# Ordering a two-layer encoder kernel at build time with operation times from a timeline simulator

## The chip, the cores and the metric

The kernel runs on one core of one Trainium2 chip. The metric is the time of one execution on the device, in microseconds (us), given as the median of several runs. Smaller is better.

## What is computed

Two layers of a hybrid bidirectional encoder for one sequence of 512 tokens (S) of width 1024 (DM), and a final RMSNorm. One layer, cut from the reference to what matters:

```
xn = rmsnorm(x, g1)
h  = xn @ W_in                       # one projection, split among four mixers
A  = gated DeltaNet, both directions: short conv + silu, l2norm(q), l2norm(k);
     chunks of 64 tokens: t_mat = I + strict_lower(k_beta k^T * decay)
     u, w = triangular_solve(t_mat, v_beta), triangular_solve(t_mat, k_beta*exp(gc))
     scan over the chunks:  v_new = u - w S
                            o = (q*exp(g)) S + a v_new
                            S = S*exp(g_last) + k_dec^T v_new
     o = rmsnorm(o) * silu(z)
B  = differential attention, two softmax maps per head
C  = windowed grouped-query attention with sinks
D  = bidirectional mLSTM, chunked
y  = sum_b sigmoid(xn @ W_gate_b) * (mixer_b @ W_branch_b)
x  = x + y @ W_out
x  = x + relu(rmsnorm(x) @ W1)^2 @ W2
```

## The kernel before

**Dense products.** Every large product is made of three passes on TensorE (PE): high part by high part, low by high, high by low. A weight block arrives by DMA on SyncE's queue in `wr`; `emit_split` (L288) has ScalarE (ACT) cast its high part into `wh` (L298) and VectorE (DVE) subtract to get the low part `wl` (L299). The activations are split in the same way (`split`, L228 on ACT and L229 on DVE). The passes stand at L398 to L400 (weights stationary, 128x256), L412 to L414 and L441 to L443 (activations stationary) and, for the MLP, L727 to L729 and L790 to L843. Their results lie in `pd`, four banks of PSUM; those of the mixers lie in `pm`, four others.

**Mixers.** A mixer is a Python generator that emits small steps. Mixer A (L1157) inverts the triangular matrices by doubling, in four pairs of groups for each layer, and scans the chunks beside it. The work of one pair, in order of dependence:

- the head: row masks `rm` on GpSimd (POOL, L1257), outer products on PE (L1261, L1263), 16 exponentials on ACT (L1267), DVE (L1272, L1274), POOL (L1273), a cast on ACT (L1276), POOL (L1277), the first block products (L1283, L1285 on DVE, L1286 on POOL), and a copy of the identity into `Q` on POOL (L1293);
- six levels: PE L1296, DVE `Q` (L1297), PE L1302 and L1304, ACT `DY` (L1306, L1307), and so to the next level;
- the tail: PE L1311, L1312, DVE `R` (L1314), ACT `q` (L1316), POOL (L1317), PE L1321, L1323, ACT `dXY` (L1325, L1326), POOL `Y` (L1328), PE L1333, DVE (L1335), PE L1339, DVE (L1340).

The scan's steps are: POOL `vb`, `kd` (L1356, L1358) and `S` (L1373), PE L1363 and L1366 (state times keys and queries), DVE L1368 to L1370, PE L1378, ACT `vn` (L1380), PE L1386 and L1396, DVE `S` (L1391) and `oc` (L1403, L1405), POOL `oc` (L1406). After the scan `head_norm` (L1134) normalizes each block of 128 tokens (POOL L1138, DVE L1140, POOL L234, DVE L1142, L1143), and `y_T` (L1146) turns it by PE (L1149).

**What sets the order.** Three things. First the order in which the program is written: `fill` (L332) takes steps from the list of dense products for as long as a table of estimated costs says, each time a mixer has emitted a step (`drive`, L347); `lockstep` (L360) takes turns among the parts of mixer A.

```
    def fill(ns):
        debt[0] += ns
        while debt[0] > 0:
            r = step()
```

Second the pools: a buffer that is still read holds up what would write it. Third the framework's scheduler, inside `tile.TileContext`. It plays the whole program at build time with an assumed duration for every operation, and puts on each engine's queue what is ready first; of what is ready, what was written earlier goes first. The result is a fixed queue for each engine, with semaphore waits. On the chip an engine takes its queue strictly in order.

**The start.** `Norm.stats` (L472 to L478) and the transposes L493 prepare the first activations. `pre` (L1094) loads small constants of a layer: `dl` (L1103), the sinks, and `cw`, the weights of the short conv, by five transfers on SyncE's queue (L1117), which DVE halves at L1119.

The change touches only the line that opens the context:

## Time and profile before

| what | before |
|---|---|
| time, median of 3 runs | 2335.07 us (2334.0 to 2337.8) |
| time of the profiled execution | 2333.33 us |
| its span, first to last instruction | 2331.6 us |
| mean granted clock of TensorE | 0.997 |
| busy: PE | 2255.5 us, 97% of the span |
| busy: DVE | 1605.4 us, 69% |
| busy: ACT | 1237.9 us, 53% |
| busy: POOL | 773.6 us, 33% |

The profile shows one execution. For each instruction, or run of like instructions, it gives the start and the duration in us, the engine, the line of the kernel, what is written and read, and in brackets how long the engine was idle before it and which engine or transfer ended that. Matmuls are pipelined: the duration of one is longer than the distance from its start to the next start, and only that distance is what the engine needs for one. A granted clock of 1.00 is 2.4 GHz, 0.50 is 1.2 GHz.

### The profile page before, as it was taken

The numbers are of one execution on the slowest core, as the hardware profiler recorded it, in microseconds if no ns is written. First come the engines' busy times: TensorE is split into PE (matmuls) and PEld (weight loads), VectorE is DVE, ScalarE is ACT, GpSimd is POOL, SyncE is SP. The second block draws the span as 40 slices with busy tenths as digits, with TensorE's granted clock in tenths as the row PEclk, the third lists the DMA queues.
The fourth block names the chain that finished last, engine by engine and source line by source line (L and its number), as shares of the span: only waits on it lengthen the run. The fifth ranks groups of instructions, "written<-read, shape, count | busy, mean of one in ns | idle before, by whom it ended". The sixth has DMA issues, their size and how long they took to land. (4 is left out here: it accounts for less than half of the span.)

```text
span 2331.6 us, 41278 instructions
## 1 busy us (share of the span) xinstructions
PE 2255.5 (97%) x15944; PEld 2014.0 (86%) x15944; DVE 1605.4 (69%) x2944; ACT 1237.9 (53%) x2827; POOL 773.6 (33%) x819
## 2 busy tenths in 40 slices
PE   7999999989999999999999999999999999999998
PEld 6879977878788989999987799878777889899998
DVE  5775547697885477677767745487877854877775
ACT  4565444766765264444445654367576633534443
POOL 1046552032332034443201655412313310444341
PEclk9999999999999999999999999999999999999999
DMA  6322131122122523233323112211322234233322
GB/s 154 94 53 64 56 95 60 55 92 81 56 66 83 162 73 120 90 104 115 107 80 91 55 56 64 91 55 55 100 73 64 64 113 136 88 99 109 100 83 91
DMA packets 234772, 200.81 MB, mean 86 GB/s; under 512 B 31824, under 2 KB 223696, under 8 KB 234576
## 3 DMA queue, kind: packets, MB, share of 16 engines
q1 hardware_dynamic: 231552, 193.09, 27.6%
q10 hardware_dynamic: 2304, 4.20, 0.5%
q8 instruction: 125, 2.05, 0.4%
q0 software_dynamic: 720, 0.89, 0.2%
q14 instruction: 71, 0.58, 0.1%
HBM read 190.25 MB, written 8.39 MB: 85 GB/s over the span
## 5 line engine op out<-in xcount | busy, mean ns | idle before, releaser
L299 DVE TENSOR_TENSOR wl<-wr,wh 128x512 fp32r<-128x512 f32 x540 | 412.1, 783 | 170.4 <-ACT wh L298 162.6
L298 ACT CAST wh<-wr 128x512 fp32r<-128x512 f32 x540 | 316.7, 620 | 222.9 <-PE pd L442 78.0
L441 PE MATMUL pd<-xh,wh 128*128 128x512 f32 (+1 forms) x768 | 307.9, 402 | 0.5 <-ACT xh L228 0.5
L442 PE MATMUL pd<-xl,wh 128*128 128x512 f32 (+1 forms) x768 | 297.3, 387 | 1.8 <-DVE xl L229 1.8
L443 PE MATMUL pd<-xh,wl 128*128 128x512 f32 (+1 forms) x768 | 298.6, 389 | 0.0
L399 PE MATMUL pd<-wl,hh 128*128 128x256 f32 x896 | 248.9, 278 | 0.0
L400 PE MATMUL pd<-wh,hl 128*128 128x256 f32 x896 | 248.8, 278 | 0.0
L398 PE MATMUL pd<-wh,hh 128*128 128x256 f32 x896 | 248.8, 278 | 0.0
L298 ACT CAST wh<-wq 128x512 fp32r<-128x512 f32 x196 | 115.2, 619 | 221.9 <-PE pd L400 95.4
L299 DVE TENSOR_TENSOR wl<-wq,wh 128x512 fp32r<-128x512 f32 x196 | 181.3, 959 | 13.6 <-ACT wh L298 13.5
L818 POOL TENSOR_TENSOR wq<-wq,wq 128x512 f32<-128x512 f32 x84 | 124.8, 1494 | 163.4 <-DVE wl L299 153.2
L443 PEld LDWEIGHTS pd<-xh,wl 128*128 128x128 f32 x768 | 145.6, 190 | 29.8
L442 PEld LDWEIGHTS pd<-xl,wh 128*128 128x128 f32 x768 | 146.2, 190 | 26.3 <-DVE xl L229 2.8
L399 PEld LDWEIGHTS pd<-wl,hh 128*128 128x128 f32 x896 | 168.7, 188 | 0.0
L400 PEld LDWEIGHTS pd<-wh,hl 128*128 128x128 f32 x896 | 168.7, 188 | 0.0
L398 PEld LDWEIGHTS pd<-wh,hh 128*128 128x128 f32 x896 | 168.2, 188 | 0.0
L441 PEld LDWEIGHTS pd<-xh,wh 128*128 128x128 f32 x768 | 145.8, 190 | 23.4 <-ACT xh L228 0.9
L686 DVE TENSOR_TENSOR x<-pd,x 128x512 f32<-128x512 f32 x124 | 85.1, 689 | 100.6 <-PE pd L400 100.5
L398 PE MATMUL pd<-wh,xh 128*128 128x256 f32 x512 | 149.6, 292 | 0.0
L399 PE MATMUL pd<-wl,xh 128*128 128x256 f32 x512 | 145.0, 283 | 0.0
L400 PE MATMUL pd<-wh,xl 128*128 128x256 f32 x512 | 143.5, 280 | 0.0
L1016 POOL TENSOR_TENSOR r<-r,r 128x512 f32<-128x512 f32 x26 | 36.1, 1390 | 301.3 <-PE pd L443 123.9
(394 smaller groups left out, 6632.6 us busy)
## 6 DMA issues: line engine op xcount, KB each, us to landing
wr<-in_w_in SPq DMA_DIRECT2D x92, 512.0 KB
wr<-in_w_mlp SPq DMA_DIRECT2D x72, 512.0 KB
wr<-in_w_gate SPq DMA_DIRECT2D x64, 512.0 KB
wq<-in_w_mlp SPq DMA_DIRECT2D x56, 512.0 KB
wr<-in_w_branch SPq DMA_DIRECT2D x32, 512.0 KB
wr<-in_w_out SPq DMA_DIRECT2D x16, 512.0 KB
x<-in_x SPq DMA_DIRECT2D x16, 256.0 KB
gsd<-gs ACTq DMA_DIRECT2D x16, 256.0 KB
```

The source lines that it names most:

```text
L298: act.copy(wh[:, k:k + n], raw[:, k:k + n])
L299: dve.tensor_tensor(wl[:, k:k + n], raw[:, k:k + n], f(wh[:, k:k + n]), op=ALU.subtract)
L398: mm(o, th, wh[:, k4, :], start=(kt == 0 and tt % 2 == 0), stop=False)
L399: mm(o, th, wl[:, k4, :], start=False, stop=False)
L400: mm(o, tl, wh[:, k4, :], start=False, stop=(kt == kts - 1 and tt % 2 == 1))
L441: mm(o, w1_, xh[kt][:, sl], start=(kt == 0 and hi_ == 0), stop=False)
L442: mm(o, w1_, xl[kt][:, sl], start=False, stop=False)
L443: mm(o, w2_, xh[kt][:, sl], start=False, stop=last)
L686: dve.tensor_tensor(d, bank.rearrange("p (t c) -> p t c", t=2), d, op=ALU.add)
L818: pool.tensor_tensor(d[:, k:k + 2], x[:, k:k + 2], y[:, k:k + 2], op=op)
L1016: pool.tensor_tensor(t, t, sh, op=ALU.add)
```

## The change

The context is opened with one more argument. It makes the scheduler take the durations that it assumes from the framework's timeline simulator, in place of its default ones.

```diff
--- before.py
+++ after.py
@@ -1738,7 +1738,7 @@
         arrays["in_" + n] = v
         args[n] = nc.dram_tensor("in_" + n, v.shape, mybir.dt.from_np(v.dtype), kind="ExternalInput").ap()
     o = nc.dram_tensor("out_0", (1, S, DM), F32, kind="ExternalOutput").ap()
-    with tile.TileContext(nc) as tc:
+    with tile.TileContext(nc, schedule_with_timeline_sim=True) as tc:
         encoder(tc, args, o)
     r = run_bass_kernel_spmd(nc, [arrays], core_ids=[0])
     return r.results[0]["out_0"]
```

No operation is added or taken away on any engine; what changes is where each stands in the queue of its engine, with the buffers and semaphores that follow from it. Three places show it.

**The start, on DVE.** `nj_32` and `nj_33` are the normalized activations of the fourth block of 128 tokens; `pm_37` holds the turned ones of the second block, `xl_21` gets their low parts, `cw_44` is the conv weights. Before:

```order
L233 TENSOR_SCALAR nv_35_179<-ntot_34_177 128x1
L478 SCALAR_TENSOR_TENSOR nj_32_173<-x_2_96,nr_36_180,g_3_99 128x512
L478 SCALAR_TENSOR_TENSOR nj_33_175<-x_2_96,nr_36_180,g_4_100 128x512
L229 TENSOR_TENSOR xl_21_143<-pm_37_185,xh_19_141 128x4x128
L229 TENSOR_TENSOR xl_22_144<-pm_38_192,xh_20_142 128x4x128
L1099 TENSOR_SCALAR gn_39_209<-gn_39_209 128x128
L1100 TENSOR_SCALAR gn_39_209<-gn_39_209 128x128
L1101 TENSOR_SCALAR gn_39_209<-gn_39_209 128x128
L229 TENSOR_TENSOR xl_21_143<-pm_59_330,xh_19_141 128x4x128
```

With the change:

```order
L1100 TENSOR_SCALAR gn_39_209<-gn_39_209 128x128
L1101 TENSOR_SCALAR gn_39_209<-gn_39_209 128x128
L1114 TENSOR_SCALAR nsink_43_227<-sink_42_225 128x8
L1106 TENSOR_TENSOR dl_40_216<-dl_40_216 128x64 x2
L1119 TENSOR_SCALAR cw_44_229<-cw_44_229 128x60
L233 TENSOR_SCALAR nv_35_179<-ntot_34_177 128x1
L1107 TENSOR_REDUCE nlam_41_218<-dl_40_216 128x1 x2
L229 TENSOR_TENSOR xl_21_143<-pm_59_330,xh_19_141 128x4x128
L1109 TENSOR_SCALAR nlam_41_218<-nlam_41_218 128x1
L478 SCALAR_TENSOR_TENSOR nj_32_173<-x_2_96,nr_36_180,g_3_99 128x512
L478 SCALAR_TENSOR_TENSOR nj_33_175<-x_2_96,nr_36_180,g_4_100 128x512
L229 TENSOR_TENSOR xl_21_143<-pm_37_185,xh_19_141 128x4x128
```

L1119, which reads what the five transfers of L1117 bring, stood eleven rows behind the low part `xl_21<-pm_37` (L229); now it stands ahead of it, and of the norm's L233 and L478. The first L442 on PE reads that low part. On PE the transposes `pm_61` (L493, four matmuls, from `nj_32`) now stand ahead of the first L442; they stood 46 dense matmuls behind it. SyncE now issues the sinks, three transfers of `cw`, `dl`, then the last two of `cw`; it was `dl`, the sinks, five of `cw`.

**The third pair of mixer A, on ACT**, from the exponentials of its head on (layer 0; layer 1 alike). Before:

```order
L1267 ACTIVATE e_423_2702<-pm_422_2699,gcol_159_1009 128x128 x4
L1267 ACTIVATE e_426_2712<-pm_425_2709,gcol_159_1009 128x128 x4
L1267 ACTIVATE e_435_2755<-pm_434_2752,gcol_159_1009 128x128 x4
L1267 ACTIVATE e_437_2763<-pm_436_2760,gcol_159_1009 128x128 x4
L1380 COPY vn_439_2773<-pm_438_2768 128x512
L1276 CAST th_440_2792<-e_423_2702 128x512
L997 COPY vx_356_2174<-pd_392_2504 128x2x128 x2
L1276 CAST th_441_2798<-e_426_2712 128x512
L298 CAST wh_470_2971<-wr_382_2385 128x512 x2
L1380 COPY vn_465_2920<-pm_464_2915 128x512
L298 CAST wh_494_3124<-wr_395_2511 128x512
L1306 CAST DY_450_2841<-pm_466_2934 128x2x64x2
```

With the change:

```order
L1267 ACTIVATE e_423_2702<-pm_422_2699,gcol_159_1009 128x128 x4
L1267 ACTIVATE e_426_2712<-pm_425_2709,gcol_159_1009 128x128 x4
L1267 ACTIVATE e_435_2755<-pm_434_2752,gcol_159_1009 128x128 x4
L1267 ACTIVATE e_437_2763<-pm_436_2760,gcol_159_1009 128x128 x4
L1380 COPY vn_439_2773<-pm_438_2768 128x512
L1276 CAST th_440_2792<-e_423_2702 128x512
L1276 CAST th_441_2798<-e_426_2712 128x512
L1380 COPY vn_465_2920<-pm_464_2915 128x512
L1306 CAST DY_450_2841<-pm_466_2934 128x2x64x2
```

The casts of weights (L298) and the reads of dense results (L997) between the steps of the head are gone; they stand earlier or later. On ACT no L298 is left from L1306 `DY_340<-pm_383`, in the fifth level of the second pair, to the tail of the third. On PE no dense matmul is left from L1302 `pm_383` to L1339 `pm_546`: 372 matmuls of mixer A in a row (184 of 128x64 and 116 of 128x128 in 16-bit floats, 64 of 128x128 in 32-bit floats, 8 of 128x512). Between the same two there were 354 dense ones. In the fourth pair there is a second such run, from L1302 `pm_606` to L1339 `pm_658`: 140 matmuls (88 of 128x64, 52 of 128x128, 16-bit), where 78 dense ones stood between them. POOL's order within these stretches is the one that it had.

**The end of the scan, on PE.** The last steps of the scan in layer 0, from L1386 `pm_670`; `pd_700` and `pd_731` are dense. Before:

```order
L1386 MATMUL pm_670_4210<-vn_669_4208,kd_661_4172 128x128 x4
L1396 MATMUL pm_671_4216<-vn_669_4208,e_560_3573 128x128 x4
L1363 MATMUL pm_674_4229<-S_666_4192,kb_69_443 128x128 x4
L1366 MATMUL pm_675_4230<-S_666_4192,qb_77_490 128x128 x4
L412 MATMUL pd_700_4322<-xh_19_141,wh_654_4130 128x512
L413 MATMUL pd_700_4322<-xl_21_143,wh_654_4130 128x512
L414 MATMUL pd_700_4322<-xh_19_141,wl_655_4131 128x512
L1378 MATMUL pm_679_4246<-vb_672_4223,Y_649_4100 128x128 x4
L412 MATMUL pd_700_4322<-xh_20_142,wh_654_4130 128x512
L413 MATMUL pd_700_4322<-xl_22_144,wh_654_4130 128x512
L414 MATMUL pd_700_4322<-xh_20_142,wl_655_4131 128x512
L412 MATMUL pd_700_4322<-xh_20_142,wh_654_4130 128x512
```

With the change:

```order
L1386 MATMUL pm_670_4210<-vn_669_4208,kd_661_4172 128x128 x4
L1396 MATMUL pm_671_4216<-vn_669_4208,e_560_3573 128x128 x4
L414 MATMUL pd_731_4498<-xh_20_142,wl_724_4443 128x512
L1363 MATMUL pm_674_4229<-S_666_4192,kb_69_443 128x128 x4
L1366 MATMUL pm_675_4230<-S_666_4192,qb_77_490 128x128 x4
L1378 MATMUL pm_679_4246<-vb_672_4223,Y_649_4100 128x128 x4
L1386 MATMUL pm_681_4253<-vn_680_4251,kd_673_4224 128x128 x4
L1396 MATMUL pm_682_4259<-vn_680_4251,e_562_3581 128x128 x4
L1363 MATMUL pm_684_4271<-S_678_4244,kb_69_443 128x128 x4
L1366 MATMUL pm_685_4272<-S_678_4244,qb_77_490 128x128 x4
L1378 MATMUL pm_688_4286<-vb_683_4268,Y_538_3456 128x128 x4
L1396 MATMUL pm_690_4293<-vn_689_4291,e_437_2763 128x128 x4
```

Four turns L1149 (`pm_720`, `pm_721`, `pm_722`, `pm_727`) follow the last row, with nothing between. From L1386 `pm_670` to the last of them there are 60 matmuls of the mixer and one dense; there were 49 dense among them. The dense matmuls that left the three runs stand earlier on PE: its queue runs ahead with dense work during the earlier pairs, and the mixer's matmuls there come later than they did. In layer 1 all three runs come again. In the MLPs PE's order is as before.

## Rows read from the trace of the kernel before

**Rows 1.** Page, busy time of each engine, and windows: 76 us of mixer A.

```profile
PE 2255.5 (97%) x15944; PEld 2014.0 (86%) x15944; DVE 1605.4 (69%) x2944; ACT 1237.9 (53%) x2827; POOL 773.6 (33%) x819
...
218.00:294.00 76.00, 75.49 (x771) 71.26 (x770) 42.39 (x72) 35.62 (x91) 44.11 (x49) 1.00 0.20 57
```

In the second row the columns are busy us and instructions of PE, PEld, DVE, ACT and POOL, then the granted clock, the DMA share and GB/s.

**Rows 2.** Waits of PE over the whole span: us in total, times, longest.

```profile
PE pm L1149 <- DVE hv L233: 10.1, 4, 3.6
PE pm L1296 <- DVE DY L1285: 6.3, 2, 3.2
...
PE pm L1149 <- DVE sq L1143: 5.0, 6, 1.4
PE pm L1544 <- ACT p L1533: 4.0, 6, 1.4
```

**Rows 3.** Timeline of the start, all engines.

```profile
17.68 7.51 SPq L1117 DMA_DIRECT2D cw<-in_gdn_conv_w  x5
...
20.83 1.41 DVE L478 SCALAR_TENSOR_TENSOR nj<-x,nr,g 128x512 f32<-128x512 f32 x2 [0.67 <-POOL nr L234]
...
22.16 1.28 DVE L229 TENSOR_TENSOR xl<-pm,xh 128x512 fp32r<-128x512 f32 x2
...
22.90 0.58 PE L442 MATMUL pd<-xl,wh 128*128 128x256 f32 x1 [1.62 <-DVE xl L229]
...
30.23 0.20 DVE L1119 TENSOR_SCALAR cw<-cw 128x60 f32<-128x60 f32 x1 [4.47 <-DMA cw<-in_gdn_conv_w]
```

**Rows 4.** Timeline of mixer A in layer 0: PE at the ends of three stretches.

```profile
294.06 0.61 PE L1339 MATMUL pm<-DY,R 128*128 128x128 f16 x6
...
320.63 0.29 PE L1302 MATMUL pm<-Q,DY 128*128 128x64 f16 x4
320.76 0.28 PE L1304 MATMUL pm<-DY,Q 128*128 128x64 f16 x4
...
345.04 0.62 PE L1339 MATMUL pm<-DY,R 128*128 128x128 f16 x8
...
353.11 1.05 PE L1386 MATMUL pm<-vn,kd 128*128 128x128 f32 x8
...
359.81 1.07 PE L1386 MATMUL pm<-vn,kd 128*128 128x128 f32 x8
...
381.04 0.60 PE L1149 MATMUL pm<-c_ident,sq 128*128 128x128 f32 x4
```

The profile records a 32-bit matmul of 128x128 twice, so x8 is a group of four.

**Rows 5.** Timeline of a level of mixer A in layer 1, DVE.

```profile
1314.81 0.74 DVE L1297 TENSOR_TENSOR Q<-pm,c_sgn 128x256 f16<-128x256 f32 x2
...
1316.51 0.42 DVE L1297 TENSOR_TENSOR Q<-pm,c_sgn 128x256 f16<-128x256 f32 x1 [0.30 <-PE pm L1296]
```

**Rows 6.** Lines L1311, L1339 in layer 0 (first start last), and a tail's timeline.

```profile
L1311 PE MATMUL pm<-DY,th x32: 216/219/231, 176.2 to 337.4; 128*128 128x128 f16 x32
...
L1339 PE MATMUL pm<-DY,R x32: 219/219/230, 181.9 to 345.4; 128*128 128x128 f16 x32
...
1376.85 0.68 DVE L1314 TENSOR_TENSOR R<-c_ident,pm 128x512 f16<-128x512 f32 x1
...
1382.99 2.04 POOL L1257 TENSOR_TENSOR rm<-RB,c_rmask 128x512 fp32r<-128x512 f32 x2
```

**Rows 7.** POOL in the third pair's head: timeline's two ends, then its window.

```profile
232.14 2.04 POOL L1257 TENSOR_TENSOR rm<-RB,c_rmask 128x512 fp32r<-128x512 f32 x2
...
254.95 2.28 POOL L1293 COPY Q<-c_identh 128x512 f16<-128x512 f16 x4
...
232.10:255.00 22.90, 18.39 (x20) 1.00 0.16 47
```

**Rows 8.** Timeline of DVE at the end of the scan.

```profile
367.55 0.76 DVE L1405 TENSOR_TENSOR oc<-pm,oc 128x256 f32<-128x256 f32 x2 [0.45 <-PE pm L1396]
```

**Rows 9.** Timeline of PE in a wait of layer 0, and the window behind it.

```profile
154.68 0.29 PE L1296 MATMUL pm<-DY,th 128*128 128x64 f16 x4 [3.17 <-DVE DY L1285]
...
155.00:175.00 20.00, 20.00 (x225) 17.98 (x225) 17.48 (x32) 11.94 (x31) 6.99 (x15) 0.91 0.40 56
```

## The prediction

> **What bounds the kernel now.** I read the page first, then the waits of TensorE (PE), then the timeline of the places that the change reorders. PE is busy for 97% of the span, DVE for 69%, ACT for 53%; in 76 us of mixer A in layer 0 PE is busy for 75.49 us, and the other engines for about half of it [rows 1]. So the end is set by PE's queue: time is lost only where the instruction at its head waits. Such waits are few: 10.1 and 5.0 us at the turns L1149, 6.3 at L1296, 4.0 at L1544 [rows 2]. The reason stands in the order of before: wherever mixer A goes through a long chain over DVE, ACT and POOL, dense matmuls lie between its steps on PE and fill the time. A chain that takes 76 us costs nothing as long as 76 us of PE work lie beside it.
>
> The change leaves every operation, so PE has the same work. What has to be priced is where its queue now offers no cover. These places are read from the new order, and their durations from the trace of before. The sum is made against the profiled execution, 2333.33 us (span 2331.6 and 1.7 around it); the median of the runs is 1.7 us above it, and I add that at the end.
>
> **Term 1, the start.** In before the fifth transfer of the conv weights lands at about 30.2 us, and DVE has waited 4.47 us for it at L1119 [rows 3]. Nothing on PE waited for that, since the first L442 had started at 22.90 [rows 3]. Now L1119 stands on DVE ahead of a norm step, of L478 twice and of the L229 that the first L442 reads. The transfers are issued one behind the other on SyncE's queue, 7.51 us for five [rows 3], and the change puts no earlier place for the last; I let it land when it did. Behind 30.4 come L478 twice (1.41 us), two L229 (1.28) and three small ones (0.7): L442 starts at some 33.9, 11 us late. About 0.5 us comes back, since four transposes are already done by then. **+10.5 us**; bounds 0 (the weights land before the wait matters) and 11.5.
>
> **Term 2, the first long run, once in each layer.** From the fifth level of the second pair to L1339 of the third, PE has 372 matmuls of the mixer and no dense one. PE's own work: 184 of 128x64 start 0.0325 us apart (four in 0.13), 116 of 128x128 0.057 apart (seven distances in 0.62 less one duration of 0.22), and 64 in 32 bits take 0.91/4 = 0.23 each, a group of four 1.05 less the overlap [rows 4]; I count the eight long ones like these. 6.0 + 6.6 + 14.7 + 1.9 = 29 us. The chain, step by step: (a) a level takes 1.7 us, from one Q of DVE at 1314.81 to the next at 1316.51 [rows 5], so the last one and two thirds of the second pair take 2.9; (b) its tail, from L1314 to the next `rm`, takes 6.1, with L1311 ahead of it 6.7 [rows 6]; (c) the head is nearly all POOL: from `rm` to the first copies of Q 22.8 us passed, in which POOL was busy for 18.4 [rows 7]; with less in its way I take 20.4; (d) six levels, 10.2; (e) the tail to L1339, 5.7 at its shortest, from 176.2 to 181.9 [rows 6]. Together 46 us. The scan of the earlier chunks goes on beside it, and its work on PE is in the 29. So PE waits for 46 - 29 = 17 us, twice: **+34 us**. Bounds for each: 0, if the chain fits into PE's own 29 us, and 47, if it takes the 76 us that it took beside dense work [rows 1, 4].
>
> **Term 3, the second run.** 140 matmuls from the third level of the fourth pair to its L1339: 88 at 0.0325 and 52 at 0.057 are 5.8 us. The chain is 3.7 levels of 1.7 and a tail of 5.7: 12.0. **+12.4 us** for two layers. Bounds for each: 0, and 18.6, by the 24.4 us from 320.63 to 345.04 that it took in before [rows 4].
>
> **Term 4, the end of the scan.** 60 mixer matmuls and a dense one, up to the last L1149: 14 groups of 0.91 us, 12.9 with the dense one. In before a step takes 6.7 us, from L1386 to L1386 (353.11 to 359.81), and from the last products of the scan (DVE's L1405 at 367.55) to the last turn at 381.04 it takes 13.5, for normalizations through POOL and DVE [rows 4, 8]. Without dense matmuls, weight splits and conv work in the way I take 6 for each of two steps and 11 for the rest: 23. **+20 us** for two layers. Bounds for each: 0, and 15, from the 27.9 us between 353.11 and 381.04 [rows 4].
>
> **Term 5, waits that go.** Where dense work is pulled ahead, mixer instructions come later on PE than they did, and so find their data ready. Of the waits at L1149 and L1544, 19.1 us [rows 2], I let half go: **-10 us**; bounds 0 and -19, and the 6.3 at L1296 may go with them.
>
> **Term 6, the clock.** After a wait of 3.17 us PE's granted clock fell from 2.4 to 1.2 GHz for a while: over the 20 us behind it the mean is 0.91, worth 1.8 us [rows 9]. In the six bare runs waits of that size are likely within the head of term 2; I take three falls, **+5 us**; bounds 0 and 10 for six. The Trainium skill, "TensorE: Matmul & The Clock Gate", section "HAM oscillation — how this bites in real kernels", goes further: short bursts of matmuls divided by waits fall to the low clock again at every burst, and pay each time. By that, the runs themselves would go at half speed, which is the second rival below; the one fall here agrees as far as it goes.
>
> **Term 7, the conv weights of layer 1.** L1119 comes nearer to its transfers there too; the wait in the first layer was 4.47 [rows 3], and PE has dense work ahead; **+2 us**, bounds 0 and 5.
>
> ACT's and DVE's casts are as many as before and only stand earlier or later; the dense matmuls that come early find them, since the pools allow three blocks ahead and PE takes longer for a block than either engine. That costs nothing while PE has dense work queued; right behind a bare run the next block must be split already, and the run itself gives the time. Sum: 10.5 + 34 + 12.4 + 20 - 10 + 5 + 2 = 74. 2333.3 + 74 + 1.7 = **2409 us**.
>
> **Rivals.** *First, the other side: the chains speed up until they fit.* The bare runs free ACT and DVE of casts. If the chain of each run needs no more than PE's own work, terms 2 to 4 are 0, the waits at L1149, L1544 and L1296 go, and the start remains: 2333.3 + 10.5 - 25.4 + 1.7 = 2320. The point from which it decides is a chain of 29 us in the first run. For it: ACT and DVE are idle for half of the 76 us [rows 1]. Against it: POOL's 18.4 us in the head [rows 7] and six levels of 1.7 [rows 5] follow each other and make 28.6 without either tail. 7%, with a good half of it above 0.2% faster and the rest near no change because part of the chains remains.
>
> *Second, the clock falls for whole runs.* If PE goes at 1.2 GHz through them, its 29 us become 58, past the chain's 46: +12; the second run's 5.8 become 11.6 and partly add, +3; the third's 12.9 become 25.8, +3. Twice 18 in place of the 5 of term 6: +31, 2440 us. For it: the fall after 3.17 us [rows 9]. Against it: most waits in levels and tails are below a microsecond, and the scan's matmuls lie between. 17%.
>
> *Third, the chains keep the pace that they had.* With the upper bounds of terms 2 to 4, 80.6 for each layer in place of 33.2, the time is 2409 + 95 = 2504. For it: the engines might have been slowed by their own order and not by waiting for PE. Against it: PE was full there [rows 1], and between `rm` and Q POOL idled only 4.5 us of 22.9 [rows 7]. 4%.
>
> That the order on the chip isn't the new one can't be: a queue is fixed when the program is built.
>
> **The numbers.** Forecast 72%, rivals 7, 17 and 4%. What a measurement of this kernel can tell from no change is about 0.2%, 4.7 us. Faster by more: 4%, from the first rival; within: 3%, also from it; slower: 93%. The range holds the forecast with its softest terms (chains a quarter shorter take 23 off term 2, 6 off term 3 and 11.5 off term 4; term 6 at 0, and term 1 with half of it, 5 each: 51 less) and reaches up past the second rival, to where term 7 is at its bound too: 2358 to 2443.
>
> **What would show it.** L442 first at 33 to 35 us, DVE waiting at L1119. From L1302 `pm_383` to L1339 `pm_546` 40 to 50 us, with PE busy for 30 of them, and waits put down to L1297, L1306, L1272, L1277 or L1286; 12 and 23 us in the other two runs; the same again in layer 1; MLP stretches as long as before. If the first run takes 60 us or more while the clock is at 1.00, the third rival is right; if it does so at 0.5, the second. If PE shows no waits in it, the first is, and the forecast is wrong.

## The result, and the profile after

The changed kernel takes 2437.91 us (median of 4 runs, 2434.16 to 2440.53) against 2336.44 us (4 runs, 2334.0 to 2338.78): a ratio of 1.0433, with a 95% interval of 1.0415 to 1.0452. It is slower, by some 101 us where 74 were forecast; the time lies inside the stated range, near its upper end.

From the page of the changed kernel: its span, the busy time of each engine (beside [rows 1]), and the granted clock in 40 slices, in tenths:

```profile
span 2432.4 us, 41245 instructions
...
PE 2290.5 (94%) x15944; PEld 2044.1 (84%) x15944; DVE 1610.0 (66%) x2944; ACT 1243.6 (51%) x2827; POOL 768.0 (32%) x819
...
PEclk9999999899999999999999999889999999999999
```

Each engine has as many operations as before and nearly the same busy time; PE's is 35 us longer for the same matmuls, and its mean granted clock is 0.981, where it was 0.997. So the 101 us are waits of PE and time at the low clock. The waits of PE over the span (us in total, times, longest), beside [rows 2]:

```profile
PE pm L1149 <- DVE sq L1143: 20.7, 8, 4.5
PE pm L493 <- DVE nj L478: 20.1, 7, 8.8
PE pm L1378 <- DVE vb L1369: 16.8, 8, 3.4
PE pm L1615 <- POOL cp L1603: 9.9, 3, 5.3
PE pm L1302 <- DVE Q L1297: 8.2, 13, 1.5
PE pm L1296 <- ACT DY L1306: 5.6, 18, 0.8
```

L1378 is a step of mixer A's scan and L1302 and L1296 are its levels. Of these, L1378, L1302 and L1296 behind ACT are new among the large ones: in before they had waited 0.5, 0.7 and 0 us in all. L1615 belongs to mixer C and had waited 3.6 us in all in before; L493, at the norms, 16.3.

For each stage I add up what PE lost: the distance from one matmul's start to the next, less the median of that distance for the same line and shape in the kernel before. That counts waits and slow clock alike. How the medians are grouped moves single sums by up to some 7 us, but the differences of A, of D and B, and of C by 3 at most. In us, both layers together:

| stage | before | changed | difference |
|---|---|---|---|
| start, up to mixer A of layer 0 | 19.8 | 23.7 | +4 |
| mixer A | 43.1 | 134.2 | +91 |
| mixers D and B | 35.4 | 15.8 | -20 |
| mixer C | 10.2 | 36.5 | +26 |
| from there to the MLPs | 3.3 | 6.8 | +3.5 |

The rest (the MLPs, and the products between the layers) differs by some 6 us the other way. A bare run is a stretch of PE's queue in which only matmuls of the mixers stand, with no dense work. The three bare runs of layer 0, as windows of the changed kernel (columns as in [rows 1]): first, second and third, then a stretch of mixer C:

```profile
281.70:335.30 53.60, 39.59 (x443) 33.46 (x441) 26.83 (x50) 24.83 (x68) 35.32 (x43) 0.90 0.04 11
380.10:392.20 12.10, 8.84 (x143) 6.55 (x141) 6.03 (x12) 9.46 (x25) 3.11 (x3) 1.00 0.14 45
407.90:442.20 34.30, 18.42 (x95) 15.49 (x95) 23.59 (x40) 7.34 (x13) 15.16 (x15) 0.72 0.06 16
...
674.00:682.60 8.60, 4.30 (x17) 3.40 (x15) 7.46 (x32) 5.41 (x21) 3.69 (x6) 0.70 0.02 6
```

They take 53.6, 12.1 and 34.3 us and lose 26.2, 6.3 and 24.0 of that; in layer 1, at 54.4, 13.2 and 32.2 us long, 26.8, 7.4 and 21.8. In before the first of these stretches took 76 us with PE busy for 75.49 of it [rows 1]. The third ends with mixer D's first steps, behind the last turn at 439.38. The second run of layer 1, and its largest wait:

```profile
1579.60:1592.60 13.00, 10.70 (x142) 8.77 (x141) 6.14 (x12) 9.45 (x25) 3.39 (x3) 0.74 0.14 42
```

```profile
PE pm L1296 <- ACT DY L1306: 1.5, 4, 0.8
```

Inside the first run, the timeline of the changed kernel (start, duration, engine, line):

```profile
285.28 0.22 PE L1311 MATMUL pm<-DY,th 128*128 128x128 f16 x1
...
292.03 2.04 POOL L1257 TENSOR_TENSOR rm<-RB,c_rmask 128x512 fp32r<-128x512 f32 x2
...
307.48 1.08 DVE L1369 TENSOR_TENSOR vb<-vb,t 128x512 f32<-128x512 f32 x1 [1.72 <-POOL vb L1356]
...
308.71 1.13 PE L1378 MATMUL pm<-vb,Y 128*128 128x128 f32 x8 [3.44 <-DVE vb L1369]
309.41 2.27 POOL L1293 COPY Q<-c_identh 128x512 f16<-128x512 f16 x4
...
310.53 0.37 PE L1302 MATMUL pm<-Q,DY 128*128 128x64 f16 x4 [0.69 <-DVE Q L1297]
...
311.50 2.06 PE L1386 MATMUL pm<-vn,kd 128*128 128x128 f32 x8
...
322.59 0.29 PE L1302 MATMUL pm<-Q,DY 128*128 128x64 f16 x4 [1.18 <-DVE Q L1297]
...
329.76 0.27 PE L1311 MATMUL pm<-DY,th 128*128 128x128 f16 x1
```

The reader is to see four pieces: a tail of 6.75 us from L1311 (285.28) to `rm` (292.03); a head of 17.4, to the first copies of `Q` at 309.41; and six levels in two halves. The first three levels, with groups of the scan between them on PE's queue (L1386, L1396, L1363, L1366, L1378 and L1396 again), take 12.1 us (310.53 to 322.59); the last three, with none, 7.2 (to 329.76), part of it at the low clock. And the clock: the group L1386 at 311.50 takes 2.06 us, where the same group takes 1.05 in [rows 4]. The largest waits of PE inside the run (281.7 to 335.3):

```profile
PE pm L1378 <- DVE vb L1369: 4.6, 2, 3.4
PE pm L1302 <- DVE Q L1297: 2.5, 5, 1.2
```

### The profile page after: what moved, and what is told of

It is laid out like the page before. It is cut to its first block, busy times and chain, and to the rows that moved or that the text cites. A ratio compares the mean times of both kernels' runs of the same rounds, so it can differ in the third digit from the quotient of the medians.

```text
span 2432.4 us, 41245 instructions
## 1 busy us (share of the span) xinstructions
PE 2290.5 (94%) x15944; PEld 2044.1 (84%) x15944; DVE 1610.0 (66%) x2944; ACT 1243.6 (51%) x2827; POOL 768.0 (32%) x819
## 5 line engine op out<-in xcount | busy, mean ns | idle before, releaser
L299 DVE TENSOR_TENSOR wl<-wr,wh 128x512 fp32r<-128x512 f32 x540 | 417.8, 805 | 164.4 <-ACT wh L298 159.8
L298 ACT CAST wh<-wr 128x512 fp32r<-128x512 f32 x540 | 307.8, 618 | 275.1 <-PE pd L442 91.8
L441 PE MATMUL pd<-xh,wh 128*128 128x512 f32 (+1 forms) x768 | 299.9, 391 | 6.8 <-ACT xh L228 2.9
L442 PE MATMUL pd<-xl,wh 128*128 128x512 f32 (+1 forms) x768 | 297.5, 387 | 0.1
L298 ACT CAST wh<-wq 128x512 fp32r<-128x512 f32 x196 | 112.2, 618 | 209.1 <-PE pd L400 93.9
L818 POOL TENSOR_TENSOR wq<-wq,wq 128x512 f32<-128x512 f32 x84 | 130.1, 1575 | 168.1 <-DVE wl L299 153.6
L299 DVE TENSOR_TENSOR wl<-wq,wh 128x512 fp32r<-128x512 f32 x196 | 152.7, 813 | 28.7 <-ACT wh L298 28.5
L442 PEld LDWEIGHTS pd<-xl,wh 128*128 128x128 f32 x768 | 145.5, 190 | 28.1 <-DVE xl L229 0.8
L843 PE MATMUL pm<-xsh,wl 128*128 128x256 f32 x448 | 126.2, 282 | 3.4 <-DVE wl L299 3.4
```

What stands on the lines that cost most here:

```text
L298: act.copy(wh[:, k:k + n], raw[:, k:k + n])
L299: dve.tensor_tensor(wl[:, k:k + n], raw[:, k:k + n], f(wh[:, k:k + n]), op=ALU.subtract)
L441: mm(o, w1_, xh[kt][:, sl], start=(kt == 0 and hi_ == 0), stop=False)
L442: mm(o, w1_, xl[kt][:, sl], start=False, stop=False)
L818: pool.tensor_tensor(d[:, k:k + 2], x[:, k:k + 2], y[:, k:k + 2], op=op)
L843: mm(o, w2_, xh[k], start=False, stop=(k == 3 and b == 1))
```

## The experiments

All are the one program, with the same instructions; what they change is the order. Each has the list of instructions of one or more engines, as they stood in one of the two kernels, packed into the file, and draws an edge from each to the one ahead of it, which fixes the order on that engine's queue and adds no wait:

```diff
+QUEUES = (
+...
+)
+def in_order(tc):
+    ins = {i.name: i for i in tc.nc.cur_bb.bb.instructions}
+    dep = mybir.DependencyInfo(mybir.DependencyClass.NoSync, mybir.DependencyReason.DATA)
+    for steps in json.loads(zlib.decompress(base64.b85decode(QUEUES))):
+...
+                tc.add_manual_dep(ins[f"I-{n}"], f"I-{last}", dep, reason="in_order")
...
     with tile.TileContext(nc, schedule_with_timeline_sim=True) as tc:
         encoder(tc, args, o)
+        in_order(tc)
```

What is not in the list the scheduler places as it likes. The list is all that differs, so only it is named below; where the last argument of the context is missing, that is said. Ratios are to the kernel before, with 95% intervals. Beside the experiments the kernel before took 2333.7 to 2334.6 us, 2 to 3 less than beside the changed kernel above (2336.44); a difference in us to the changed kernel is uncertain by that much, and ratios are the safer comparison.

**Mixer A alone, undone.** List: all engines, mixer A's stretch in the order of before.

> The changed kernel with all queues pinned to the order of before within mixer A's stretch (everything written from mixer A's first step to mixer D's first), in both layers; start, D, B, C and the MLPs are the scheduler's. Theory Q: the 45 us in each layer go, 2438 - 90 = 2348 us. Then mixer C tells two theories apart: if its 14 us in each layer come from dense work that had been used up in A and D, they go too, and it is 2320 us if D and B keep their gain of 10, about 2340 if not; if they come from how D, B and C themselves are ordered, they stay, and it is 2348 us. Rival E: over 2390 us.

2350.64 us, 1.0075 (1.0059 to 1.0092). PE loses 51.4 us in mixer A in place of 134.2, and 13.0 in D and B; mixer C still loses 40.0. So A's loss is A's order: undone, it gives back 87 us, or 84 by the ratios. C's 26 are not a consequence of A. The wait of C in this run:

```profile
PE pm L1615 <- POOL cp L1603: 9.6, 2, 5.3
```

**Mixer A alone, done.** List: all engines, mixer A's stretch in the order of the changed kernel; the context without its argument.

```diff
-    with tile.TileContext(nc, schedule_with_timeline_sim=True) as tc:
+    with tile.TileContext(nc) as tc:
```

> The mirror of a_before: the kernel before (default times in the scheduler) with all queues pinned to the order of the changed kernel within mixer A's stretch, both layers; the rest is the scheduler's. Theory Q: A alone costs its 45 us in each layer, 2334 + 90 = 2424 us; runs of 54, 12 and 34 us bare of dense work. If dense work drained in A is also missed later, D, B and C lose 5 to 10 us more: up to 2445 us. Rival (A's loss comes from what precedes it, the late start): under 2390 us.

2421.1 us, 1.0378 (1.0361 to 1.0395). A loses 129.7, D and B 39.9, C 10.2, as in before. The mirror gives the same sum from the other side, 87 us, and with the rest in its default order the dense work that A uses up is not missed later.

**The start.** List: all engines, all that is written ahead of mixer A.

> The changed kernel with all queues pinned to the order of before for everything that is written ahead of mixer A of layer 0's first step at L1231 (the norm, the small constants with L1119, and the first dense products); the rest is the scheduler's. Theory Q: L442 starts at about 23 us in place of 30.3, all else is shifted by that: 5 to 7 us less than the changed kernel, 2431 us. Rival (the start's wait is made good later, since the mixers' chains and not PE set the pace there): within 2 us of the changed kernel.

2433.87 us, 1.0432 (1.0416 to 1.0447). That is 4.0 us under the changed kernel, but the ratio is the same (1.0433), and the two profiled executions differ by 1.4 us (spans of 2431.0 and 2432.4). L442 starts at 21.9, as meant, and mixer A begins 6.5 us earlier; but mixer C of layer 0 loses 22.3 in place of 18.0. So the start's wait is there and goes, and no gain at the end is shown: between 0 and 4 us. The rival fits at least as well as theory Q.

**D, B and C.** List: all engines, from mixer D's first step to the end of the mixers.

> The changed kernel with all queues pinned to the order of before from mixer D's first step to the end of the layer's mixers; the start and mixer A are the scheduler's. By the stage sums of the changed kernel, C's 13.5 us in each layer go and the 10 that D and B had gained go too: 2438 - 27 + 20 = 2431 us if each stage loses by its own order (theory C). Rival U (the dense work drained in mixer A is what the later stages lack): D, B and C lose more than in before, over 2450 us.

2444.82 us, 1.0471 (1.0457 to 1.0486). C falls to 14.0, but D and B lose 45.2, more than in before, and 15.3 come behind C, most of it where the next norm begins (L493 and the first products of the MLP). The time lies between the two theories, and each holds for a part: C's loss goes with the order of D, B and C, and D and B lose more instead.

**Start, A and C.** List: all engines, start, mixer A's stretch and mixer C's.

> The changed kernel with all queues pinned to the order of before in the start, in mixer A's stretch and in what is written from mixer C's first step to the end of the layer's mixers; D and B (and the MLPs) are the scheduler's. In a_before D and B lost 6.5 us in each layer against 17.5 in before, and C 20 against 5. Theory C (mixer C's loss is its own order): C falls back to 5 and D and B keep their gain: 2334 - 22 = 2312 us, faster than both kernels. Rival U (D and B gain only by using up dense work that C then lacks): C or the end of B loses the same again, 2325 to 2345 us.

2348.49 us, 1.006 (1.0047 to 1.0072). A is at 51.0, D and B at 21.8, C at 22.9 and 12.5 come behind C. Theory C falls. Rival U holds in kind, at 3 us above its range: D and B gain 14, and C loses 13 more than in before although it stands in its old order. The 12.5 behind C, at the next norm again, are in neither theory. Nothing is faster than the kernel before.

**PE's queue alone, undone and done.** List: PE, the whole program, in the order of before; then PE in the order of the changed kernel, with the context without its argument.

> The changed kernel with PE's queue pinned to the order that it had before; the queues of DVE, ACT, POOL and SyncE are still the scheduler's with the simulator's times. Theory Q (the lost time is PE's own queue: mixer steps with no dense work between them): PE's order takes back all but the late conv weights on DVE at the start; 2335 to 2350 us, no stretch of PE without dense work over 8 us in mixer A, run from L1302 pm_383 to L1339 pm_546 70 to 80 us. Rival E (the other engines' queues cost it: weight splits and mixer D's casts ahead of the chain's steps; PE's bare stretches only show that): over 2390 us, with waits of PE at L1378, L1149 and L1296 as in the changed kernel.

> The kernel before with PE's queue alone pinned to the order of the changed kernel; the scheduler has its default times for the other queues. Theory Q: 2415 to 2440 us, the three bare stretches as long as in the changed kernel (54, 12 and 34 us). Rival E: under 2380 us, bare stretches some 40, 10 and 20 us long, since the chain's steps are no longer behind other work.

2398.63 us, 1.0279 (1.0263 to 1.0294), and 2493.99 us, 1.0689 (1.0673 to 1.0705). Theory Q misses both times. Rival E's time for the first came true, but not its waits (L1378 waits for 0.7 us in all there), and for the second it misses as well. PE's order takes back 39 us and leaves 65, and the changed order of PE with the other engines' default order is worse than the changed kernel by 56.

In the second of the two, mixer A loses 132 us, as much as in the changed kernel, and its bare runs are nearly as long as there (50.7, 12.8 and 30.0 us in layer 0). The first of them:

```profile
283.00:333.70 50.70, 38.69 (x443) 33.02 (x442) 27.09 (x50) 24.48 (x68) 35.59 (x43) 0.93 0.04 12
```

So PE's changed order is by itself enough for A's whole loss; the 56 us more are lost in D and B (some 30) and in C (some 19), where PE's order was made for other queues. But undoing PE's order alone does not undo A's loss: in the first of the two, mixer A loses 86.4, half way between 43.1 and 134.2, though no stretch bare of dense work is longer than 6.6 us there. What is left in layer 0's A, as waits and on the timeline:

```profile
PE pm L1302 <- DVE Q L1297: 9.3, 7, 3.3
PE pm L1149 <- POOL hr L234: 6.1, 1, 6.1
...
392.61 2.26 DVE L299 TENSOR_TENSOR wl<-wr,wh 128x512 fp32r<-128x512 f32 x2
...
396.72 4.33 POOL L234 TENSOR_TENSOR hr<-hv,c_col 128x4 f32<-128x4 f32 x4
...
399.50 0.69 DVE L1142 TENSOR_TENSOR sq<-oc,hr 128x512 f32<-128x512 f32 x1
```

DVE splits two halves of a weight block (L299) between the last product of the scan and its norm, and the four norms then go through together. L1142 starts only at 399.50, while PE's order asks for the first turn some 6 us earlier.

**Which other engine.** Lists: PE and DVE; PE and POOL; PE, DVE and ACT; each for the whole program in the order of before.

> The changed kernel with the queues of PE and DVE pinned to the order of before; ACT, POOL and SyncE are the scheduler's. In pe_before mixer A still lost 21 us more in each layer than in before, at L1302 behind DVE's L1297 and at L1149 behind the norms. Theory D (DVE's queue costs that, its weight splits L299 and its batched norms standing ahead of what PE waits for): 2334 to 2350 us. Rival P (POOL's queue costs it: the four L234 behind all L1138): over 2375 us, with the waits at L1149 unchanged.

> The same with the queues of PE and POOL pinned to the order of before; DVE, ACT and SyncE are the scheduler's. Theory D: 2385 to 2400 us, as pe_before. Rival P: 2345 to 2360 us, the late start left.

> The changed kernel with the queues of PE, DVE and ACT pinned to the order of before; POOL and SyncE are the scheduler's. pe_before was at 2399 us, pe_dve_before at 2376, 42 over before. Theory T (ACT's casts standing at other places than those that DVE's and PE's order counts on make the rest): 2334 to 2345 us. Rival (POOL's batched L234 and SyncE's later loads make it): over 2360 us.

| queues listed | time, us | ratio (interval) | lost in A | lost in C |
|---|---|---|---|---|
| none (changed kernel) | 2437.91 | 1.0433 (1.0415 to 1.0452) | 134.2 | 36.5 |
| PE | 2398.63 | 1.0279 (1.0263 to 1.0294) | 86.4 | 21.6 |
| PE, POOL | 2394.36 | 1.0263 (1.0248 to 1.0279) | 87.3 | 22.7 |
| PE, DVE | 2376.14 | 1.0181 (1.0165 to 1.0196) | 56.0 | 23.8 |
| PE, DVE, ACT | 2337.22 | 1.0014 (1.0005 to 1.0024) | 42.6 | 12.6 |

Undone one after the other, PE's order gives back 39 us, DVE's a further 22, ACT's a further 39; POOL's next to PE's 4, and what is left with POOL's and SyncE's is 3 (1.0014). These shares belong to this sequence: no run undid DVE's or ACT's order without PE's, and the run above shows that PE's order alone can cost as much in A as all of them. The list of DVE leaves out some steps of mixer C (L1596), which stand elsewhere than in before. Rival P falls by its second run (2394 us where it said 2345 to 2360); the first came out over 2375, as it said, but the waits at L1149 did not stay: 30.6 us in all with PE's order, 16.2 with DVE's too. Theory D is right in kind for mixer A, but at 2376 us it missed its 2334 to 2350, for ACT's order carries as much; theory T holds.

**One bare run at a time.** Lists: PE's stretch from L1302 `pm_383` to L1339 `pm_546`, dense matmuls included, with the mixer's steps on DVE, ACT and POOL; then the same from L1386 `pm_670` to the last L1149.

> The changed kernel with PE's queue from L1302 pm_383 to L1339 pm_546, dense matmuls included, and the mixer's steps of DVE, ACT and POOL in that stretch pinned to the order of before, in both layers. The built order has dense matmuls in that run again, and 228 mixer matmuls without any just ahead of it. Theory S (dense work is a stock; what is held back is missed just ahead): the run of 54 us loses its 26 us of waits, and a bare chain of some 35 us over 12 us of PE's work costs 20 to 23: 2425 to 2436 us. Theory I (the stretches are independent): 2438 - 2 x 26 = 2386 us.

> The same for the end of the scan alone: from L1386 pm_670 to the last L1149 pm_727, 49 dense matmuls included, pinned to the order of before in both layers. The built order has 196 mixer matmuls bare just ahead, in place of 140. Theory S: the end of the scan falls from 34 to about 29 us with dense work in it and loses 18 us less; two scan steps more in the bare run ahead cost 8 to 14: 2410 to 2430 us. Theory I: 2438 - 2 x 18 = 2402 us or less.

2421.72 us, 1.0375 (1.036 to 1.0391), and 2413.52 us, 1.0341 (1.0326 to 1.0356): 16 and 24 us back, where the runs lose 53 and 46. The windows of the stretches ahead, first of the one, then of the other kernel:

```profile
206.10:236.30 30.20, 22.42 (x252) 17.52 (x251) 13.08 (x25) 16.86 (x50) 22.64 (x28) 0.82 0.07 19
```

```profile
368.40:393.00 24.60, 19.27 (x227) 16.42 (x226) 11.74 (x22) 11.00 (x29) 12.63 (x16) 0.86 0.13 44
```

In the first, a new bare run of 30.1 us stands ahead of the mended one. In the second the 12.1 us of the second run have become 24.5. Dense work that is held back for one chain is missing in the chain ahead of it. Theory S holds (for the first run its 2425 to 2436 was 3 us too high), theory I falls.

Not tried: DVE's or ACT's order without PE's; and mixer A's levels ahead of the scan's steps on PE within the first run, which would test directly what the steps cost there. The part of the loss that each wait has of itself, and not by the low clock that follows it, was not taken apart by a run either.

## Why the prediction was right, and where it was off

The main mechanism is the one forecast: PE's queue has long chains of mixer A without cover, and waits there. That the loss stands in mixer A is shown from both sides (mixer A alone, undone and done), and that PE's order is enough for it by the run with PE's queue done. The first rival, that the chains would fit into PE's own work, falls: PE waits in all six runs. The third, chains at their old pace, falls too: the first run takes 53.6 us, not 76. Of the signs that were named, L442 came earlier than 33 to 35, and the first run took more than its 40 to 50 (53.6 and 54.4). That the time still lies in the range is in part luck: one loss of 26 us was not in the sum at all, and misses of either sign cancel in the rest.

*Term 1, the start* (+10.5). The transfers land sooner than in [rows 3], and DVE is through L1119 at 27.3, not 30.4; L442 starts 7.4 us late, not 11. The timeline of the changed kernel:

```profile
17.05 3.68 SPq L1117 DMA_DIRECT2D cw<-in_gdn_conv_w  x3
20.77 0.72 SPq L1103 DMA_DIRECT2D dl<-in_diff_lambda  x1
21.54 1.26 SPq L1117 DMA_DIRECT2D cw<-in_gdn_conv_w  x2
...
25.36 0.36 DVE L1106 TENSOR_TENSOR dl<-dl 128x64 f32<-128x64 f32 x2 [4.67 <-DMA dl<-in_diff_lambda]
27.09 0.19 DVE L1119 TENSOR_SCALAR cw<-cw 128x60 f32<-128x60 f32 x1 [1.37 <-DMA rb<-in_mlstm_gate_b]
...
29.12 1.09 PE L493 MATMUL pm<-c_ident,nj 128*128 128x128 f32 x4 [7.68 <-DVE nj L478]
30.29 0.58 PE L442 MATMUL pd<-xl,wh 128*128 128x256 f32 x1
```

SyncE took 4.94 us for the five transfers in place of 7.51. The wait is the one forecast, in two pieces: 4.67 us at L1106 for `dl`, which the sum had left out, and 1.37 more at L1119. The profile names a transfer of `rb` for the second; L1119 reads `cw` alone, and its last transfer went out right ahead of that one, so I take it for `cw`. In the stage sums the start costs 4 us, and undoing it shows no gain at the end (the experiment on the start).

*Term 2, the first run* (17 each, measured 26.2 and 26.8). PE's own work was 27.7 us by the same count (29 forecast). Steps (a) and (b) hold: two levels in 3.3 us and a tail of 6.75. Step (c) was put at 20.4 and is 17.4. The step that failed is (d): six levels at 1.7 were to take 10.2 and took 19.2. The prediction said that the scan "goes on beside it, and its work on PE is in the 29". It does not go on beside it: PE takes its queue in order, and the scan's steps stand between the levels. In the 12.1 us of the first three levels six groups of the scan stand on PE, some 5.5 us at 0.91 each by the figure of the prediction; the first two ran in part at the low clock (L1386 takes 2.06 in place of 1.05), and two of the six waited for inputs of their own (1.17 and 0.44 us). Three levels at 1.7 and 5.5 us are already 10.6. So by these rows the two chains add where they alternate, and the largest waits in the whole run, 4.6 us at L1378, are a step of the scan that the prediction had not named among its signs. This is read from the timeline, three levels with scan steps against three without; no run tested it alone.

*Term 3, the second run* (6.2 each): 6.3 and 7.4; the run took 12.1 us in layer 0, where 12.0 were forecast, and 13.2 in layer 1, part of it at the low clock (0.74). There is no scan in it.

*Term 4, the end of the scan* (10 each, measured 24.0 and 21.8). 23 us were forecast for the run; up to the last turn it takes some 33. The two steps of the scan were to take 6 us each and take about 9 (from 406.15 to L1386 at 415.24, then to the last L1396 at 424.59); the rest was to take 11 and takes 14.8, to 439.38. The rows of the changed kernel:

```profile
408.81 1.96 DVE L299 TENSOR_TENSOR wl<-wr,wh 128x512 fp32r<-128x512 f32 x2
...
412.71 1.84 PE L1378 MATMUL pm<-vb,Y 128*128 128x128 f32 x8 [2.59 <-DVE vb L1369]
...
415.24 2.08 PE L1386 MATMUL pm<-vn,kd 128*128 128x128 f32 x8 [0.68 <-ACT vn L1380]
...
424.59 1.16 PE L1396 MATMUL pm<-vn,e 128*128 128x128 f32 x8 [0.68 <-ACT vn L1380]
...
430.29 1.09 PE L1149 MATMUL pm<-c_ident,sq 128*128 128x128 f32 x4 [4.54 <-DVE sq L1143]
...
439.38 1.08 PE L1149 MATMUL pm<-c_ident,sq 128*128 128x128 f32 x4 [0.24 <-DVE sq L1143]
```

I had taken weight splits and conv work out of the way; DVE's new queue has a split of 1.96 us right ahead of the first step, and in both steps groups ran at the low clock (L1386 takes 2.08 where it took 1.05). A bare stretch on PE says nothing of the other engines' queues; they have to be read too. The runs on single engines say the same of the whole: with PE's order undone first, DVE's and ACT's carry 61 of the 101 us, and the prediction put the new places of their casts at nothing.

*Term 5, waits that go* (-10): of the waits named, the 10.1 at L1149 behind `hv` and the 4.0 at L1544 are gone altogether, while the 5.0 at L1149 behind `sq` grew to 20.7, which is part of term 4. D and B lose 20 us less in all. Half was too careful.

*Term 6 and the second rival, the clock* (+5). The granted clock is 0.90 in the first run and 0.72 in the third, 0.70 in the stretch of mixer C: it fell to 1.2 GHz twice in each of them in layer 0, behind waits (the first fall at mixer C comes at 672.4, before that window, behind one of 1.50 us at 671.13). The windows of the four falls in the two runs:

```profile
308.00:316.00 8.00, 6.60 (x59) 6.32 (x60) 3.36 (x8) 1.81 (x5) 5.59 (x10) 0.79 0.00 0
324.00:332.00 8.00, 6.75 (x92) 5.90 (x91) 3.63 (x8) 4.64 (x15) 0.00 (x0) 0.57 0.00 1
412.00:424.00 12.00, 8.96 (x48) 8.34 (x48) 5.37 (x8) 0.64 (x2) 3.90 (x4) 0.72 0.14 43
428.00:444.00 16.00, 7.88 (x25) 5.33 (x26) 13.99 (x23) 7.93 (x15) 6.46 (x6) 0.57 0.00 0
```

PE's busy time in each (the first figure behind the length) by the share of the clock that was missing is 1.4 + 2.9 + 2.5 + 3.4 = 10 us in layer 0, an estimate of what the clock took in these two runs, where 2.5 were forecast for a layer. It is part of the losses of terms 2 and 4. The rival said that whole runs would go at half speed and cost 18 in a layer; by that estimate it was about half. Its time, 2440 us, is near the measured one for another reason (mixer C, below). The Trainium skill's rule ("TensorE: Matmul & The Clock Gate", section "HAM oscillation — how this bites in real kernels"), that bursts divided by waits pay the slow clock again each time, agrees with these falls in part: the clock fell again and again, but not at every wait. And long waits are not needed: the second run stayed at 1.00 in layer 0, but in layer 1 it shows 0.74, with no wait in it over 0.8 us and PE busy for 10.70 of 13.00 us.

*Term 7* (+2): DVE waited 2.6 us for layer 1's conv weights, with dense work on PE; no wait of PE comes from it.

*Not priced: mixer C*, +26 us, which is nearly the whole gap of 28 between forecast and result. The prediction has no term for it: it looked for stretches without cover in mixer A alone, and its sentence that ACT's and DVE's casts "only stand earlier or later" and cost nothing went for all stages behind A. The largest wait in C of layer 0, in the changed kernel:

```profile
679.41 0.69 PE L1615 MATMUL pm<-c_ident,cp 128*128 128x128 f32 x2 [4.30 <-POOL cp L1603]
```

It stands where mixer C begins, in a stretch without dense work, and is 4.30 of the 18 us that C loses in this layer; the rest is the low clock and shorter waits. Which queue C's loss comes from stays open: it falls from 36.5 to 21.6 with PE's old order, and to 12.6 only when DVE's and ACT's are undone too. The other misses nearly cancel: terms 2 to 4, the clock among them, gave 112 in place of 66 plus 5; against that stand the waits of before that went from the same stages (A's other waits 22 in place of 43), ten more in D and B, and six in the start.

## What to carry to other kernels

An order made from other durations is not one edit but one on every engine: read the new queues of all engines for what stands ahead of the steps that a chain needs, and count the work without cover on the bound engine in every stage, not only where it is longest. Where two chains alternate on one in-order queue, count their times as added, as the first run's rows suggest. To find which stage an order's cost belongs to, fix the order of one stage at a time, from both sides: here mixer A gave 87 us either way. Stages that share a stock of dense work do not come apart so well (what D and B gained, C lost), nor do engines: one engine's order made for another's queues gave the worst time of all (2494 us).

## What was not expected of the hardware

The same five transfers of the conv weights held SyncE's queue for 7.51 us in one kernel and for 4.94 in the other; a part of that only moved, for the transfer right behind them took 1.34 and 2.43. And the clock fell on a queue that was busy for three quarters of the time or more: in the first run the rows show 0.90 over 53.6 us, with no wait there longer than 3.44, and in the second run of layer 1 0.74 over 13 us, with none over 0.8.
